# SwiGLU gate and up as two by two blocks with seven products, the down projection in three pieces

## The chip, the cores and the metric

One core of a Trainium2 chip runs the whole kernel. The metric is the device time of one execution in microseconds. Five engines work side by side, each through its own queue in order: TensorE (PE in the profile: matmuls; PEld: the loads of their weights), VectorE (DVE), ScalarE (ACT), GpSimd (POOL) and SyncE (SP, which issues most DMAs). Matmuls write PSUM, eight banks that VectorE and ScalarE read.

## The reference

One decoder layer for 512 prompt tokens and 64 sample tokens (T = 576) of width 1024: a mixer (Mamba-2 heads and mLSTM heads), cross-attention over a memory, and SwiGLU, each between two RMS norms and added to the stream x. The change is in the last part:

```python
x = x + _rms(o) * g_post_x
u = _rms(x) * g_pre_ffn
f = (jax.nn.silu(u @ w_gate) * (u @ w_up)) @ w_down    # 1024 -> 2816 -> 1024
x = x + _rms(f) * g_post_ffn
```

All is float32.

## The kernel before

Activations lie features by tokens: eight tiles of 128 features, 576 tokens. A float32 product is made of three matmuls in the faster fp32r type: each operand is split into a high and a low part, and hi·hi, lo·hi and hi·lo are added in PSUM. A weight tile (128 output features, 1024 input features) is one load of 512 KB into `raw` (two buffers); `split_w` (L170) then makes `whi` by a cast on ScalarE (L177) and `wlo` by a subtraction, the first `cut` columns on VectorE and the others on GpSimd (L184). With `acc` the low part is instead a negated copy by ScalarE (L181), to which a DMA issued by GpSimd adds the weight once more from memory (L182). `whi` and `wlo` have three buffers each, with `NWX` more in a pool `wx` for one stage. `weights` (L1058) keeps the last few split tiles, so that both halves of the tokens use one split.

`gemm` (L191) runs 24 matmuls for one tile and one half of the tokens: eight weight tiles times three (L197, L198, L199). The tokens are cut in `HALVES`, 256 and 320.

The part around the change, in order:

- `xo` (L1364): output projection of the cross-attention for eight tiles, first half, then second half in the order `XO1`. `chain` (L1378) adds the normed result to x and splits it into `u3h` and `u3l`; `pre_sums` adds up squares for the next norm, whose factor comes as `rb3`.
- Tiles 0 to 3 of gate and up (`products` L1398, `hidden` L1404): the first half of the tokens while VectorE still works on the second half of x, then the second half. `hidden` multiplies both products by `rb3` (the norm's factor is applied after the matmul), takes silu of the gate on ScalarE, multiplies on GpSimd and splits the result into `hh` and `hl`.
- The loop over tiles 4 to 21 (`NFFN` is 22), both halves each.
- `down` (L1472): for each of eight output tiles and each half 66 matmuls over all 22 hidden tiles in one PSUM bank, then a square for the last norm and a scaled copy.
- The end: the factor of the last norm for the second half, the last two down products of the first half around it, the additions to x (`post_add`), transposes of the first half (`final0`) and the output DMAs.

The program is written in order, and a scheduler orders each engine's queue by a simulated timeline in which earlier lines have priority; it places tiles into their buffers and adds the waits. `issue_after` holds instructions behind a given one on their engine.

## Time and profile before

| | us |
|---|---|
| median of 3 runs | 1146.4 |
| lowest, highest | 1144.42, 1146.73 |
| profiled execution | 1144.03 |
| its span | 1142.3 |
| TensorE busy (matmuls) | 1127.8 |
| VectorE busy | 631.9 |
| ScalarE busy | 507.7 |
| GpSimd busy | 319.2 |

The span runs from the first instruction to the last; the profiled execution's own time has another 1.7 us around it. The granted clock of TensorE was 0.999 of full speed. Busy times are unions of the time in which an engine had an instruction running, and matmuls overlap each other, so a matmul's own duration is longer than the distance to the next one. In the DMA view a row names destination and source, issuing queue, count, KB of one and the median us from issue to landing.

### The profile page before, as it was taken

What the parts mean: (1) busy time and instruction counts of PE and PEld (TensorE: products, weight loads), DVE (VectorE), ACT (ScalarE), POOL (GpSimd) and SP (SyncE); (2) the same over time, 40 slices, a digit from 0 to 9 for tenths busy, and PEclk for the clock granted to TensorE, in tenths of its full rate; (3) what the DMA queues carried; (4) which work ended last, traced back from release to release, by engine and by line L of the source; (5) the groups of instructions that cost most, each with busy time, mean ns of one, the idle gap of its engine ahead of it and who ended that gap; (6) DMA issues with size and microseconds to landing.
All of it is one profiled execution on the core that took longest, in us unless ns stands there. A gap on an engine that the chain in (4) does not pass through costs nothing.

```text
span 1142.3 us, 21407 instructions
## 1 busy us (share of the span) xinstructions
PE 1127.8 (99%) x8633; PEld 1079.5 (95%) x8633; DVE 631.9 (55%) x1266; ACT 507.7 (44%) x930; POOL 319.2 (28%) x349
## 2 busy tenths in 40 slices
PE   9999999999999999999999999999999999999997
PEld 8999888898998999999888899999999999999997
DVE  6796774558777762568444547834434444311225
ACT  6877533355554463655344455522223232232222
POOL 1333443313122111101343200224433443331330
PEclk9999999999999999999999999999999999999999
DMA  6685565445554432544577733412222233422332
GB/s 213 156 171 126 130 167 165 140 111 142 162 161 123 128 111 84 166 167 157 193 248 249 266 124 97 154 56 78 89 92 75 75 92 93 152 72 82 102 102 97
DMA packets 48023, 153.38 MB, mean 134 GB/s; under 512 B 5260, under 2 KB 9484, under 8 KB 47412
## 3 DMA queue, kind: packets, MB, share of 16 engines
q1 hardware_dynamic: 42164, 139.43, 38.1%
q0 software_dynamic: 5760, 12.59, 6.8%
q8 instruction: 67, 1.10, 0.4%
q14 instruction: 32, 0.26, 0.1%
HBM read 135.54 MB, written 16.45 MB: 133 GB/s over the span
## 4 chain that ended last, share of the span: by engine, by line
PE 87%; DMA 4%; DVE 3%; ACT 3%; issue 1%; SPq 0%; POOL 0%; POOLq 0%; DVEq 0%; ACTq 0%
PE ps_in L197 5%; PE ps_in L199 5%; PE ps_in L198 5%; PE ps_u L199 4%; PE ps_g L199 4%; PE ps_dn L197 4%; PE ps_g L198 4%; PE ps_u L198 4%; PE ps_g L197 4%; PE ps_u L197 4%; PE ps_dn L199 4%; PE ps_dn L198 4%; PE ps_o L199 3%; PE ps_o L197 3%; PE ps_o L198 3%; PE ps_v L770 2%
## 5 line engine op out<-in xcount | busy, mean ns | idle before, releaser
L177 ACT CAST whi<-raw 128x1024 fp32r<-128x1024 f32 (+1 forms) x166 | 171.6, 1036 | 212.9 <-issue 50.4
L184 DVE TENSOR_TENSOR wlo<-raw,whi 128x512 fp32r<-128x512 f32 (+1 forms) x158 | 144.8, 916 | 164.0 <-ACT whi L177 163.3
L184 POOL TENSOR_TENSOR wlo<-raw,whi 128x512 fp32r<-128x512 f32 (+1 forms) x82 | 139.2, 1698 | 237.5 <-ACT whi L177 233.9
L197 PE MATMUL ps_in<-uh,whi 128*128 128x320 f32 (+1 forms) x544 | 165.3, 304 | 0.0
L199 PE MATMUL ps_in<-uh,wlo 128*128 128x320 f32 (+1 forms) x544 | 162.8, 300 | 0.2 <-DVE wlo L184 0.2
L198 PE MATMUL ps_in<-ul,whi 128*128 128x320 f32 (+1 forms) x544 | 162.2, 298 | 0.0
L197 PEld LDWEIGHTS ps_in<-uh,whi 128*128 128x128 f32 x544 | 103.0, 189 | 2.2 <-issue 0.8
L199 PEld LDWEIGHTS ps_in<-uh,wlo 128*128 128x128 f32 x544 | 102.9, 189 | 2.1 <-issue 1.3
L197 PE MATMUL ps_u<-u3h,whi 128*128 128x256 f32 (+1 forms) x352 | 104.3, 296 | 0.0
L199 PE MATMUL ps_g<-u3h,wlo 128*128 128x256 f32 (+1 forms) x352 | 104.3, 296 | 0.0
L199 PE MATMUL ps_u<-u3h,wlo 128*128 128x256 f32 (+1 forms) x352 | 104.3, 296 | 0.0
L197 PE MATMUL ps_g<-u3h,whi 128*128 128x256 f32 (+1 forms) x352 | 104.3, 296 | 0.0
L198 PE MATMUL ps_g<-u3l,whi 128*128 128x256 f32 (+1 forms) x352 | 104.3, 296 | 0.0
L198 PE MATMUL ps_u<-u3l,whi 128*128 128x256 f32 (+1 forms) x352 | 104.2, 296 | 0.0
L197 PE MATMUL ps_dn<-hh,whi 128*128 128x320 f32 (+1 forms) x352 | 104.2, 296 | 0.0
L199 PE MATMUL ps_dn<-hh,wlo 128*128 128x320 f32 (+1 forms) x352 | 103.9, 295 | 0.0
L198 PE MATMUL ps_dn<-hl,whi 128*128 128x320 f32 (+1 forms) x352 | 103.8, 295 | 0.0
L198 PEld LDWEIGHTS ps_in<-ul,whi 128*128 128x128 f32 x544 | 103.1, 189 | 0.7
L199 PEld LDWEIGHTS ps_g<-u3h,wlo 128*128 128x128 f32 x352 | 66.8, 190 | 0.1
L199 PEld LDWEIGHTS ps_u<-u3h,wlo 128*128 128x128 f32 x352 | 66.8, 190 | 0.1
L198 PEld LDWEIGHTS ps_u<-u3l,whi 128*128 128x128 f32 x352 | 66.8, 190 | 0.0
L197 PEld LDWEIGHTS ps_g<-u3h,whi 128*128 128x128 f32 x352 | 66.8, 190 | 0.0
(591 smaller groups left out, 2952.3 us busy)
## 6 DMA issues: line engine op xcount, KB each, us to landing
raw<-win SPq DMA_DIRECT2D x35, 512.0 KB, 3.8
raw<-wgate SPq DMA_DIRECT2D x23, 512.0 KB, 3.5
raw<-wup SPq DMA_DIRECT2D x22, 512.0 KB, 3.6
raw<-wdown SPq DMA_DIRECT2D x18, 512.0 KB, 3.5
raw<-wout SPq DMA_DIRECT2D x17, 512.0 KB, 3.6
kva<-kc SPq DMA_DIRECT2D x16, 512.0 KB, 6.6
kva<-vc SPq DMA_DIRECT2D x16, 512.0 KB, 7.1
raw<-wxq SPq DMA_DIRECT2D x13, 512.0 KB, 3.6
```

Source lines behind the costliest of these rows:

```text
L177: A.copy(hi[:, :n], raw[:, :n])
L184: e.tensor_tensor(lo[:, a:b], raw[:, a:b], hi[:, a:b].bitcast(F32), op=ALU.subtract)
L197: mm(ps, wh, ah, start=i == 0, stop=False)
L198: mm(ps, wh, al, start=False, stop=False)
L199: m = mm(ps, wl, ah, start=False, stop=i == len(tiles) - 1)
L770: m = mm(o, ah, lo[:, j:j + 256], start=False, stop=k == KT - 1, skip_group_check=True)
```

## The change

**Halves.** From the output projection of the cross-attention up to the end of gate and up the tokens are cut 288 and 288 (`EHALVES`), with the norm's transposes in overlapping chunks (`ECHUNKS`).

**Tiles 0 to 3** stay as they were, in another order: tile 3 comes first for its first half, and it is computed for both halves once more behind the sums of blocks.

**Sums of blocks.** x is stored to memory and then scaled in place by gain and norm factor. With four blocks B11, B12, B21, B22 (two halves of the input features by two halves of the tokens) VectorE and ScalarE make the high and low parts of seven operands, `b11`, `b21`, `t1` to `t4`, `b22`.

**Pairs.** Tiles 4 to 21 are taken two at a time. For gate and for up of each pair, a `Pair` loads both weight tiles, forms sums of their blocks on VectorE and splits four operands: `w1` (high part by ScalarE, low part by negation and an accumulating DMA), `w2`, `w3` (one half of its low part by an accumulating DMA) and `w4` of half width. Seven products of 12 matmuls, 288 columns each, replace the 96 matmuls of two tiles and two halves. They go into three PSUM banks; three intermediate sums are copied out by ScalarE and added by VectorE (`done`). On TensorE the order is `early` (two products), `late` of the pair before (two), `mid` (three). GpSimd has no tensor work left here: silu's product is on VectorE.

**Down** goes in three pieces, after hidden tiles 0 to 7, 8 to 15 and 16 to 21. The first piece is copied from PSUM to `f2`, the others are added to it by VectorE. Each piece starts with three partial products that leave out the last two hidden tiles, with `late` of the last pair behind the first of them. The last piece runs all second halves, then all first halves, with the last norm and the additions to x between.

**Room.** Ten small tiles of the mixer and one of the attention move from long-lived pools to those of their stages, and `NWX` goes from 4 to 3.

```diff
@@ -28,6 +28,9 @@
 CHUNKS = [(0, 128), (128, 128), (256, 128), (384, 128), (512, 64)]
 HALVES = [(0, 256), (256, 320)]
 HCHUNKS = [CHUNKS[:2], CHUNKS[2:]]
+EHALVES = [(0, 288), (288, 288)]
+ECHUNKS = [[(0, 128), (128, 128), (160, 128)], [(288, 128), (416, 128), (448, 128)]]
...
-NWX = 4
+NWX = 3
...
-    CT = cp.tile([P, 5, 104], F32, name="CT")
-    cumst = cp.tile([80, T], BF16, name="cumst")
...
+    CT = ml.tile([P, 5, 104], F32, name="CT")
+    cumst = ml.tile([80, T], BF16, name="cumst")
...
-        xo(j, 0, wx if 2 < j < 7 else None)
-    post_rstd(0, ssq, rb, "px0")
+        xo(j, 0, wx if 3 < j < 7 else None)
+    rstd_rows(rstd_cols([ssq], ECHUNKS[0], "px0", alloc=B0), ECHUNKS[0], rb, B0)
     for n_, j in enumerate(XO1):
         xo(j, 1)
         if n_ < 2:
             chain(0, range(4 * n_, 4 * n_ + 4))
         if n_ in (3, 5):
-            pre_sums(0, x, ssq3, range(2 * n_ - 6, 2 * n_ - 2))
-    hh = [SL0("hh0"), SL(2, "hh1", F32R), None]
-    hl = [SL(1, "hl0", F32R), SL(4, "hl1", F32R), None]
-    def products(j, i, up, pool=None, cut=CUT):
-        t0, n = HALVES[i]
+            sums(0, range(2 * n_ - 6, 2 * n_ - 2))
+    S.dma_start(x_d[:, :, E[0]], x[:, :, E[0]])
...
+    psg, m = products(3, 0, 0)
     with tc.issue_after(m.ins):
-        rc = rstd_cols([ssq3], HCHUNKS[0], "p30", alloc=B1)
-    psu, m = products(0, 0, 1, wx, 1024)
+        rc = rstd_cols([ssq3], ECHUNKS[0], "p30", alloc=B1)
+    psu, m = products(3, 0, 1)
...
+    hidden(3, 0, psg, psu)
+    psg, m = products(0, 0, 0, wx)
...
+    hidden(2, 1, psg, psu)
+    for j in (1, 0):
         ffn(j, 1)
     wxs.close()
+    S.dma_start(x_d[:, :, E[1]], x[:, :, E[1]])
     fp = ctx.enter_context(tc.tile_pool(name="ffn", bufs=1, reuse_waits="tile"))
-    tp_ = fp
-    hh[2], hl[2] = [fp.tile([P, 6, T], F32R, name=k) for k in ("hh2", "hl2")]
-    S.dma_start(x_d, x)
-    for j in range(4, NFFN):
-        ffn(j, 0)
-        ffn(j, 1)
-    f = SL(3, "f_ffn")
-    x2 = SL(5, "x2")
+    b4 = SL(4, "b4", F32R, (P, 16, 288))
+    b5 = bx.tile([P, 16, 288], F32R, name="b5", tag="b5")
+    (B11, B12), (B21, B22) = [[x[:, 4 * k:4 * k + 4, c] for c in E] for k in range(2)]
+    for i in range(2):
+        for k in range(KT):
+            V.scalar_tensor_tensor(x[:, k, E[i]], x[:, k, E[i]], PAR("g_preffn", k), rb3[:, E[i]], op0=ALU.mult, op1=ALU.mult)
+    def parts(t_, i, src):
+        hi, lo = [t_[:, 4 * k:4 * k + 4, :] for k in (i, i + 1)]
+        split(hi, lo, src)
+        return hi, lo
+    def minus(out, a, b):
+        V.tensor_tensor(out, a, b, op=ALU.subtract)
+    b11 = parts(b4, 0, B11)
+    minus(B11, B12, B11)
+    t1 = parts(b5, 2, B11)
+    minus(B11, B22, B11)
+    t2 = parts(b5, 0, B11)
+    b21 = parts(b4, 2, B21)
+    minus(B12, B22, B12)
+    minus(B21, B21, B11)
+    ffn(3, 0)
+    ffn(3, 1)
+    b3, bf = SL(3, "b3", F32R, (P, 16, 288)), fp.tile([P, 8, 288], F32R, name="bf")
+    t3, t4, b22 = parts(b3, 0, B12), parts(b3, 2, B21), parts(bf, 0, B22)
+    gs = SL(5, "gs", F32, (P, 16, 288))
+    sw = [gs[:, 8 + 4 * i:12 + 4 * i, :].rearrange("p a b -> p (a b)")[:, 0:1024] for i in range(2)]
+    f2 = SL(1, "f_ffn")
...
+    class Pair:
+        def __init__(s, j, up, hh, hl):
+            s.j, s.up, s.hh, s.hl = j, up, hh, hl
+            src = I["wup" if up else "wgate"]
+            r1 = wp.tile([P, 1024], F32, name="raw", tag="raw", bufs=2)
+            r2 = fp.tile([P, 1024], F32, name="rawx", tag="rawx", bufs=2)
+            st_ = sw[up]
+            S.dma_start(r1, src[j])
+            S.dma_start(r2, src[j + 1])
+            a, b = slice(0, 512), slice(512, 1024)
+            hl_ = lambda p=wp, k=("whi", "wlo"), n=1024, m=3: [p.tile([P, n], F32R, name=q, tag=q, bufs=m) for q in k]
+            w1, w2, w3 = hl_(), hl_(), hl_()
+            w4 = hl_(fp, ("w4h", "w4l"), 512, 2)
+            neg = lambda w, c: A.activation(w[1][:, c], w[0][:, c].bitcast(F32), AF.Copy, scale=-1.0)
+            A.copy(w1[0], r1)
+            neg(w1, slice(0, 1024))
+            G.dma_start(w1[1], src[j], accum_op=ALU.add)
+            V.tensor_tensor(st_[:, b], r2[:, a], r2[:, b], op=ALU.add)
+            V.tensor_tensor(st_[:, a], st_[:, b], r1[:, a], op=ALU.subtract)
+            V.tensor_tensor(r2[:, a], r1[:, a], r2[:, a], op=ALU.subtract)
+            V.tensor_tensor(r1[:, b], r1[:, b], st_[:, a], op=ALU.subtract)
+            split(*w2, st_)
+            A.copy(w3[0], r2)
+            neg(w3, b)
+            G.dma_start(w3[1][:, b], src[j + 1, :, b], accum_op=ALU.add)
+            V.tensor_tensor(w3[1][:, a], r2[:, a], w3[0][:, a].bitcast(F32), op=ALU.subtract)
+            split(*w4, r1[:, b])
+            s.w = w1, w2, w3, w4
+            s.ps = None
+        def bank(s):
+            return (MP if s.up else GP)("ps_u" if s.up else "ps_g")[:, :288]
+        def mul(s, ps, w, i, b, start=True):
+            hi, lo = s.w[w]
+            for k in range(4):
+                wh, wl = [t_[:, 512 * i + k * P:512 * i + k * P + P] for t_ in (hi, lo)]
+                mm(ps, wh, b[0][:, k, :], start=start and k == 0, stop=False, skip_group_check=True)
+                mm(ps, wh, b[1][:, k, :], start=False, stop=False, skip_group_check=True)
+                m = mm(ps, wl, b[0][:, k, :], start=False, stop=k == 3, skip_group_check=True)
+            return m
+        def tmp(s, k):
+            return tp_.tile([P, 288], F32, name=k, tag=k, bufs=3)
+        def done(s, a, i, ps, more=None):
+            g = gates(s.j)[a][i]
+            if not s.up:
+                if more is not None:
+                    V.tensor_tensor(g, ps, more, op=ALU.add)
+                A.activation(g, ps if more is None else g, AF.Silu)
+                return
+            if more is not None:
+                t_ = s.tmp("t2")
+                V.tensor_tensor(t_, ps, more, op=ALU.add)
+                ps = t_
+            V.tensor_tensor(g, g, ps, op=ALU.mult)
+            k = (s.j + a) % 8
+            split(s.hh[:, k, E[i]], s.hl[:, k, E[i]], g)
+        def early(s):
+            s.x, y = s.bank(), s.bank()
+            s.mul(s.x, 0, 0, b11)
+            c = s.tmp("t1")
+            A.copy(c, s.x)
+            s.mul(y, 0, 1, b21)
+            s.done(0, 0, y, c)
+        def mid(s):
+            s.mul(s.x, 1, 0, t2, False)
+            s.c2, c3 = s.tmp("t1"), s.tmp("t1")
+            A.copy(s.c2, s.x)
+            s.z = s.bank()
+            s.mul(s.z, 1, 1, t1)
+            s.mul(s.x, 2, 0, t3, False)
+            A.copy(c3, s.x)
+            s.done(1, 1, s.z, c3)
+        def late(s):
+            s.mul(s.x, 2, 1, t4, False)
+            s.done(1, 0, s.x)
+            s.mul(s.z, 3, 0, b22, False)
+            s.done(0, 1, s.z, s.c2)
+    def pairs(js, hh, hl):
+        last = None
+        for j in js:
+            for up in range(2):
+                p = Pair(j, up, hh, hl)
+                p.early()
+                if last:
+                    last.late()
+                p.mid()
+                last = p
+        return last
+    def down_part(c, nk, j, i, ps, w, k0, k1):
+        t0, n = HALVES[i]
+        return gemm(ps, [(*w, nk)], act(hh), act(hl), t0, n, k0, k1)
+    def down_chunk(c, nk, order, last, w_of, evac):
+        ps, n1 = {}, nk - 2
+        def get(j, i):
+            if (j, i) not in ps:
+                ps[j, i] = (GP if len(ps) < 3 or len(ps) % 2 else MP)("ps_dn")[:, :HALVES[i][1]]
+            return ps[j, i]
+        for n_, (j, i) in enumerate(order[:3]):
+            down_part(c, nk, j, i, get(j, i), w_of(j), 0, n1)
+            if n_ == 0:
+                last.late()
+        for n_, (j, i) in enumerate(order):
+            p = get(j, i)
+            m = down_part(c, nk, j, i, p, w_of(j), n1 if n_ < 3 else 0, nk)
+            evac(n_, j, i, p, m)
+    def ev_first(n_, j, i, ps, m):
+        t0, n = HALVES[i]
+        A.copy(f2[:, j, t0:t0 + n], ps)
+    def ev_add(n_, j, i, ps, m):
+        t0, n = HALVES[i]
+        V.tensor_tensor(f2[:, j, t0:t0 + n], f2[:, j, t0:t0 + n], ps, op=ALU.add)
+    for c, (js, ev) in enumerate((((4, 6), ev_first), ((8, 10, 12, 14), ev_add))):
+        if c:
+            hh, hl = SL0("hh%d" % c), SL(2, "hl%d" % c, F32R)
+        last = pairs(js, hh, hl)
+        w_of = lambda j: weights(("d", j, c), I["wdown"][j, :, 1024 * c:1024 * c + 1024], cut=1024)
+        down_chunk(c, 8, [(j, i) for j in range(8) for i in (1, 0)], last, w_of, ev)
+    hh, hl = SL0("hh2"), SL(2, "hl2", F32R)
+    last = pairs((16, 18, 20), hh, hl)
...
+    wdh = SL(4, "wdh", F32R, (P, 6, 768))
+    wdl = bx.tile([P, 16, 288], F32R, name="wdl", tag="b5").rearrange("p a b -> p (a b)").rearrange("p (j c) -> p j c", c=768)
+    x2 = SL(3, "x2")
     ssqf = ssq_tile("ssqf")
     rb = rb_tile("pf_rb")
-    def down_ws(j, cut):
-        return [(*weights(("d", j, q), I["wdown"][j, :, 1024 * q:1024 * q + 128 * m], 128 * m, cut=min(cut, 128 * m)), m)
-                for q, m in enumerate((8, 8, 6))]
-    HH = lambda k, t0, n: hh[k // 8][:, k % 8, t0:t0 + n]
-    HL = lambda k, t0, n: hl[k // 8][:, k % 8, t0:t0 + n]
-    def down_evac(j):
-        def ev(t0, n, ps):
-            add_sq(ph, ssqf, ps, j, n, t0=t0)
-            A.activation(f[:, j, t0:t0 + n], ps, AF.Copy, scale=PAR("g_postffn", j))
-        return ev
-    def down(j, i, cut=CUT):
-        gemm2(down_ws(j, cut), HH, HL, down_evac(j), "ps_dn", [i], GP if i else MP)
+    kept = {}
+    def w_of(j):
+        if j not in kept:
+            src = I["wdown"][j, :, 2048:2816]
+            kept[j] = split_w(src, 768, 768) if j > 5 else split_w(src, 768, to=(wdh[:, j, :], wdl[:, j, :]))
+        return kept[j]
+    def down_evac(n_, j, i, ps, m):
+        t0, n = HALVES[i]
+        fj = f2[:, j, t0:t0 + n]
+        V.tensor_tensor(fj, fj, ps, op=ALU.add)
+        add_sq(ph, ssqf, fj, n_, n, t0=t0)
+        A.activation(fj, fj, AF.Copy, scale=PAR("g_postffn", j))
+    down_chunk(2, 6, [(j, 1) for j in (6, 7, 0, 1, 2, 3, 4, 5)], last, w_of, down_evac)
+    S.dma_start(x2, x_d)
...
+    for n_, j in enumerate(range(8)):
+        ps = (MP if n_ % 2 else GP)("ps_dn")[:, :256]
+        m = down_part(2, 6, j, 0, ps, w_of(j), 0, 6)
+        down_evac(n_, j, 0, ps, m)
+        if n_ == 1:
+            with tc.issue_after(m.ins):
+                rc = rstd_cols([ssqf], HCHUNKS[1], "pf1", alloc=B0)
+        if n_ == 3:
+            with tc.issue_after(m.ins):
+                rstd_rows(rc, HCHUNKS[1], rb, B0)
+            for k in range(8):
+                post_add(1, f2, x2, rb, [k], False)
+                if k % 2:
+                    S.dma_start(O["y1"][:, k - 1:k + 1, :], x2[:, k - 1:k + 1, 256:T])
```

More of the change, by code (lines that the diff above doesn't have):

```diff
@@ L1430, in build @@
[L1430 to L1444 removed]
+        rstd_rows(rc, ECHUNKS[0], rb3, B1)
```

122 lines of the change are left out of this document (53 added, 69 removed).

## The prediction

> **What bounds the kernel now.** I read the page's engine line and its chain first, then stretches of the span, then single instructions of the SwiGLU and the down projection.
>
> ```profile
> span 1142.3 us, 21407 instructions
> PE 1127.8 (99%) x8633; PEld 1079.5 (95%) x8633; DVE 631.9 (55%) x1266; ACT 507.7 (44%) x930; POOL 319.2 (28%) x349
> ...
> PE 87%; DMA 4%; DVE 3%; ACT 3%; issue 1%; SPq 0%; POOL 0%; POOLq 0%; DVEq 0%; ACTq 0%
> ```
>
> TensorE is busy 99% of the 1142.3 us and carries 87% of the chain. The next fence gives stretches: us, then busy time (and instructions) of each engine.
>
> ```profile
> core 0: us, PE busy (x) PEld busy (x) DVE busy (x) ACT busy (x) POOL busy (x), PEclk, DMA share, GB/s
> 659.00:745.00 86.00, 85.95 (x659) 84.91 (x656) 59.88 (x125) 46.69 (x94) 9.95 (x11) 1.00 0.39 126
> ...
> 760.00:985.00 225.00, 225.00 (x1693) 225.00 (x1693) 94.68 (x140) 64.97 (x105) 87.52 (x70) 1.00 0.27 82
> ```
>
> Row 760 to 985 is the loop over tiles 4 to 21 of gate and up, which the change rewrites. TensorE is busy in all 225.00 us; VectorE in 94.68 (42%), ScalarE in 64.97 (29%), GpSimd in 87.52. Nothing but the matmuls sets the time there, so fewer matmuls are worth their full price as long as the three other engines, which get more to do, never make TensorE wait. Row 659 to 745 is the stage ahead (the cross-attention output, tiles 0 to 3): VectorE is at 59.88 of 86.
>
> Price of a matmul, from the starts of three timeline rows (start, duration, instruction):
>
> ```profile
> 990.21 0.31 PE L197 MATMUL ps_dn<-hh,whi 128*128 128x320 f32 x1
> ...
> 999.89 0.28 PE L197 MATMUL ps_dn<-hh,whi 128*128 128x256 f32 x1
> ...
> 1007.73 0.31 PE L197 MATMUL ps_dn<-hh,whi 128*128 128x320 f32 x1
> ```
>
> Each stretch between them is 22 weight tiles by three matmuls, 66 in all. 320 columns: (999.89 - 990.21)/66 = 0.1467 us. 256 columns: (1007.73 - 999.89)/66 = 0.1188. A width of 288 isn't in the trace; it lies halfway, and I take 0.1327, between those ends.
>
> **The matmuls.** A pair of tiles of one kind (gate or up) costs 2 tiles x 24 matmuls x (0.1467 + 0.1188) = 12.74 us. The seven products are 7 x 4 weight tiles x 3 = 84 matmuls of 288 columns: 84 x 0.1327 = 11.15 us. That is 1.59 less, for nine pairs of tiles and two kinds: 18 x 1.59 = 28.7 us. But the new code computes tile 3 for its first half twice (once at the start, once more in the call after the block sums): 48 x 0.1327 = +6.4 us. The down projection keeps its matmuls, only their order changes. Net on TensorE: **-22.3 us**. All else is waits that come back.
>
> **Load of the other engines, per pair of one kind.** Rows: count, busy us, mean ns.
>
> ```profile
> L177 ACT CAST whi<-raw 128x1024 fp32r<-128x1024 f32 x34 | 35.7, 1050 | 63.6 <-issue 34.3 <-PE ps_g L198 27.3 <-PE ps_u L198 2.1
> ...
> L189 DVE TENSOR_TENSOR hl<-t,hh 128x320 fp32r<-128x320 f32 x18 | 26.4, 1467 | 1.6 <-ACT hh L188 1.6
> ...
> L1408 DVE TENSOR_TENSOR t<-ps_g,p_rb 128x320 f32<-128x320 f32 x17 | 8.3, 490 | 22.0 <-PE ps_g L199 22.0
> ...
> L1410 ACT ACTIVATE t<-t 128x320 f32<-128x320 f32 x17 | 7.9, 467 | 0.0
> ...
> L1408 DVE TENSOR_TENSOR t<-ps_g,p_rb 128x256 f32<-128x256 f32 x18 | 7.4, 412 | 0.3 <-PE ps_g L199 0.3
> ...
> L189 DVE TENSOR_TENSOR hl<-t,hh 128x256 fp32r<-128x256 f32 x17 | 7.2, 424 | 23.5 <-ACT hh L188 23.5
> ```
>
> ```profile
> L184 DVE TENSOR_TENSOR wlo<-raw,whi 128x512 fp32r<-128x512 f32 x22 | 15.9, 721 | 59.0 <-ACT whi L177 59.0
> ```
>
> ```profile
> L184 DVE TENSOR_TENSOR wlo<-raw,whi 128x1024 fp32r<-128x1024 f32 x14 | 17.1, 1223 | 13.8 <-ACT whi L177 13.8
> L1039 DVE SCALAR_TENSOR_TENSOR u3l<-x,par,u3h 128x320 fp32r<-128x320 f32 x8 | 4.4, 598 | 0.0
> ```
>
> ```profile
> L181 ACT ACTIVATE wlo<-whi 128x512 fp32r<-128x512 f32 x32 | 19.8, 626 | 0.3
> ...
> L181 ACT ACTIVATE wlo<-whi 128x1024 fp32r<-128x1024 f32 x8 | 8.4, 1054 | 0.1
> ```
>
> VectorE per pair: six passes of 512 columns (four sums of blocks, two low parts; 721 ns each), one of 1024 (1223 ns), so 5.5 us of weights; a 288-wide pass over PSUM lies between 412 and 490 ns, 0.45: three for gate; three, four products and four low parts for up. So 6.9 us for gate and 10.5 for up, mean 8.7 of 11.15 (78%). ScalarE: four passes of 1024 (1050 and 1054 ns), two of 512 (626 ns), three PSUM copies and four silu or casts (467 ns at 320 columns, so about 0.44): 8.5 us (76%). Both below TensorE, with the up pair close on VectorE; I cost this load at nothing, covered by the gate pair's slack of 4 us, and if that cover goes, VectorE's excess is the price. GpSimd loses its tensor passes in this loop. The two low-part rows (1467 ns at 320 columns, 424 at 256) show VectorE being slowed when GpSimd runs beside it, so this side can also gain a little; off the path, zero.
>
> **The new wait.** There are three buffers of weight parts, and each pair now uses all three (w1, w2, w3). The first block's low part goes ScalarE copy, ScalarE negation, then an accumulating DMA by GpSimd. The same chain stands in the input projection:
>
> ```profile
> 29.50 1.06 ACT whi L177
> 30.59 1.06 ACT wlo L181
> ```
>
> ```profile
> 31.97 1.06 POOL L182 DMA_DIRECT2D wlo<-win  x1 [3.80 <-ACT wlo L181]
> ```
>
> ```profile
> wlo<-win POOLq DMA_DIRECT2D x24, 256.0 KB, 5.7
> ...
> wlo<-win POOLq DMA_DIRECT2D x8, 512.0 KB, 5.6
> ```
>
> ```profile
> DMA to landing us min/median/max: 3.9/5.8/9.3
> ```
>
> The copy starts at 29.50, the negation at 30.59 and the DMA at 31.97 (0.32 after the negation's end); landing takes 5.6 us in the median at 512 KB, 3.9 to 9.3 over all forty. So from a free buffer to a usable low part: 31.97 - 29.50 + 5.6 = 8.1 us. The order on TensorE is first part of pair p (24 matmuls), last part of p-1 (24), middle of p (36), first part of p+1. w1 comes free after the first 24, so its successor has 60 matmuls, 60 x 0.1327 = 7.96 us, plus two before the low part is first read (0.27): 8.2. That is a tie. When a landing is 5.6 or less nothing waits; when it is slower all of it shows, since TensorE's queue is in order and the last part of p, which is ready sooner, stands behind. Bounds: 0 (landing 5.6) to 9.3 - 5.7 = 3.6 us per pair. Half of the landings are above the median; with an average excess of some 1.2 us there, I take 0.6, nearer zero as the median row is. Fifteen times a pair follows a pair; for twelve of them this holds: **+7.2**.
>
> The other three are the second pair of each group (8, 16 and 4 begin a group after other work). There no last part stands between: the buffer has 36 matmuls, 4.78 + 0.27 = 5.05 us, for the 8.1, so 3.1 us short, unless the scheduler puts the last part of the first pair ahead, which fills it. I take half: 3 x 1.55 = **+4.7** (0 to 9.3).
>
> On the Trainium skill: "DMA: Bandwidth & Descriptors", Anatomy of one DMA (the GpSimd path), gives about 2.0 us plus bytes over 436 GB/s, an estimate of 3.2 us for 512 KB. This trace disagrees for the accumulating form: 5.6 us, and 5.7 for half the bytes, and only the shortest of forty comes near. By the skill's figure both items above would be about 0 and the sum -17.3. I go by the rows.
>
> **From tiles 0 to 3 into the pairs.** VectorE gets 16 scalings (below 598 ns, 0.55: 8.8 us), seven low parts of 1152 columns (1.22 x 1152/1024 = 1.38: 9.6) and four differences (5.5), 23.9 us. The last three of the low parts (4.1) stand behind tile 3's last matmul, which frees the two u3 buffers. Ahead of that, from the second half's norm on, lie 192 matmuls (25.5 us) with 8 us of VectorE work of their own, and idle time in the stage before (26 of 86 us). About 19.8 to place in 17.5 plus a part of that idle time: it nearly fits. After the release the first pair needs two block sums, a cast and a low part (0.72 x 2 + 1.05 + 1.22 = 3.7) against 24 matmuls (3.2), behind tile 3's own evacuation. **+3** (0 to 10).
>
> **Tail.** The long passes over x stay, 16 in number:
>
> ```profile
> 1126.07 3.31 DVE L1031 TENSOR_TENSOR f_ffn<-f_ffn,pf_rb 128x320 f32<-128x320 f32 x8 [0.65 <-ACT pf_rb L248]
> 1129.30 3.30 DVE L1032 TENSOR_TENSOR x<-x,f_ffn 128x320 f32<-128x320 f32 x8
> ```
>
> 3.31 + 3.30 = 6.6 us. They now share VectorE with two passes (0.42 each) for each of four evacuations: 10.0 us against four groups of 18 matmuls at 0.1188, 8.6. With one more addition in the last evacuation: **+2** (0 to 4). The added sums of the first two down pieces (0.45 each) hide behind 24 matmuls (2.8 us or more). One more reload of an output weight hides in the stage that has VectorE and ScalarE idle; uncovered it is 2.3. The extra accumulating traffic, 18 x 768 KB = 13.8 MB, goes into a loop whose DMA share is 0.27.
>
> **Sum.** -22.3 + 7.2 + 4.7 + 3 + 2 = **-5.4 us**. The profiled execution took 1144.0 (span 1142.3), the median of the runs is 1146.4, 0.2% above. Carried to the median: **1141.0**. About 0.2% (2.3 us) is what a measurement of this kernel can tell from no change.
>
> **Rivals.** First, the cycle of the w1 buffer as the bound, slower than before. w3 of a pair asks for a buffer earlier in the program than w1 of the next. If it takes the one that the first part frees, w1 must wait for the one that the last part frees halfway: 12 matmuls in, 48 left, 6.37 + 0.27 = 6.6 us for 8.1. That is 1.5 more, twelve times: +18, 1159. It decides from 0.45 us per pair upwards (5.4/12): beyond that the change loses. For it: the tie above, and a median landing that half of the DMAs exceed; against it: if w3 is early, the last part is ready early too, and could be placed first.
>
> Second, VectorE as the bound of the transition: 23.9 us found covered only by halves, 10 us more than I took, 1151. For it: 78% load with in-order queues behind waiting evacuations; against it: 26 idle us in the stage ahead.
>
> Third, the gain comes through: all landings near the shortest (3.9), the chain 6.4, no wait in the twelve, 1.35 in the three: -22.3 + 4 + 3 + 2 = -13.3, 1133. Against it stands the median of forty, nearly 2 us longer. The Trainium skill's figure, named above, would have it so.
>
> That the change doesn't do what it says is out: the counts of matmuls are in the code.
>
> **How the numbers follow.** Forecast 0.45 (its own range 1130 to 1152, from 0 to 1.5 us per pair), first rival 0.30 (1150 to 1168), second 0.12 (1146 to 1158), third 0.13 (1127 to 1136). Range 1127 to 1163, which leaves out the far end of the first rival and little else. Faster by over 0.2% (below 1144.1): 0.7 of the forecast plus the third, 0.45. Within: 0.18 of the forecast, 0.08. Slower: 0.47.
>
> **What would show it.** The pair loop's matmuls at 84 per pair, 288 wide, starting 0.133 us apart (a width dearer than halfway would undo the saving directly). Then TensorE's idle time in that loop, in the list of waits, put down to the accumulating DMA into the low part: 7 us right, 0 the third rival, 20 and more the first. Idle time at the first pairs put down to ScalarE or VectorE instead, over 8 us, is the second. The forecast is wrong if VectorE or ScalarE is above 90% in the loop, or if the stages ahead of 650 us, which only have tiles moved between pools, take another time.

## The result, and the profile after

The changed kernel takes 1184.3 us (median of 4 runs, 1179.05 to 1188.19) against 1146.6 for the kernel before in the same session: 1.033 times as long, interval 1.0287 to 1.0373. The forecast was 1141, its range ended at 1163. The profiled execution took 1183.3 us.

The page of the profile after, engine line:

```profile
span 1181.5 us, 21257 instructions
PE 1123.5 (95%) x8471; PEld 1067.5 (90%) x8471; DVE 722.1 (61%) x1437; ACT 594.2 (50%) x1082; POOL 227.8 (19%) x289
```

TensorE has 162 matmuls fewer and is busy 4.3 us less, but in a span that is 39.2 us longer. With the 22.3 us that the matmuls should save, some 61.5 us of loss are to be found. Stretches of the span after, cut at the borders of the stages: the last products of x and tiles 0 to 3; group 1 (four pairs); down; group 2 (eight pairs); down; group 3 (six pairs); down and the end. Columns as before: us, busy time of each engine, granted clock, DMA share.

```profile
core 0: us, PE busy (x) PEld busy (x) DVE busy (x) ACT busy (x) POOL busy (x), PEclk, DMA share, GB/s
655.00:774.20 119.20, 115.38 (x868) 111.24 (x867) 84.96 (x165) 60.51 (x114) 16.69 (x14) 1.00 0.43 138
774.20:831.70 57.50, 45.16 (x303) 42.62 (x302) 38.31 (x60) 32.33 (x53) 8.35 (x9) 0.91 0.49 118
831.70:887.40 55.70, 55.70 (x423) 55.70 (x422) 17.78 (x23) 17.62 (x30) 0.86 (x1) 1.00 0.34 97
887.40:995.10 107.70, 91.64 (x638) 89.34 (x637) 56.24 (x98) 57.28 (x98) 13.01 (x15) 0.95 0.54 127
...
1050.90:1122.40 71.50, 64.37 (x470) 62.50 (x469) 39.89 (x69) 41.74 (x71) 9.52 (x11) 1.00 0.55 124
1122.40:1156.30 33.90, 32.90 (x239) 32.64 (x238) 18.27 (x33) 15.94 (x31) 0.00 (x0) 1.00 0.38 136
1156.30:1181.50 25.20, 17.02 (x134) 15.91 (x132) 14.34 (x39) 8.44 (x18) 2.83 (x3) 0.84 0.26 94
```

The three groups are 300, 636 and 468 matmuls long (the last 36 of each lie within the next down piece), which at 0.1333 us is 40.0, 84.8 and 62.4. So group 1 loses 17.5 us, group 2 22.9 and group 3 9.1, together 49.5. In group 2, 16.1 of it is idle time (107.70 - 91.64). The other 6.8 are busy time above the price of the matmuls: about 4.5 in three stretches at a lower clock (one of them is shown below; the row's clock is 0.95), the rest at the eight restarts after waits. Group 3, with a clock of 1.00, has 2.0 of such busy time too (64.37 - 62.4). The down stretch between them is at its price. From 1122.4 to the end are 59.1 us for matmuls worth 43.0, so 16.1 are something else; from the first down product of the kernel before to its end it was 152.1 - 140.2 = 11.9. That makes 4.2 more at the end. The remaining 7.8 us lie ahead of the first pair.

TensorE's list of waits (us in total, times, longest):

```profile
PE ps_u L1540 <- DMA wlo<-wup: 14.2, 6, 3.5
PE ps_g L1540 <- DMA wlo<-wgate: 8.7, 6, 2.2
PE ps_g L1538 <- ACT whi L191: 7.5, 4, 4.6
```

The accumulating DMA is waited for 22.9 us, where the prediction had put 7 for its forecast and "20 and more" for the first rival. The third line is ScalarE's; 4.55 of its 7.5 us are at the first pair and 1.51 at the third. With VectorE's low parts (1.13 and 1.06) and three shorter waits, group 1 has 10.2 us of waits for these two engines, and the prediction's sign for the second rival was over 8. So both signs were there.

One cycle of group 2. First TensorE's timeline, then ScalarE's and GpSimd's (start, duration):

```profile
922.61 0.32 PE L1538 MATMUL ps_u<-b,whi 128*128 128x288 f32 x1
922.77 0.29 PE L1539 MATMUL ps_u<-b,whi 128*128 128x288 f32 x1
926.41 0.40 PE L1540 MATMUL ps_u<-b,wlo 128*128 128x288 f32 x1 [3.35 <-DMA wlo<-wup]
926.65 0.29 PE L1538 MATMUL ps_u<-b,whi 128*128 128x288 f32 x1
...
927.71 0.67 PE L1540 MATMUL ps_u<-b,wlo 128*128 128x288 f32 x2
928.18 0.44 PE L1538 MATMUL ps_u<-b,whi 128*128 128x288 f32 x1
...
931.07 0.33 PE L1538 MATMUL ps_g<-b,whi 128*128 128x288 f32 x1
```

```profile
914.46 1.05 ACT L1523 CAST whi<-rawx 128x1024 fp32r<-128x1024 f32 x1 [0.50 <-ACT hh L191]
...
916.42 1.05 ACT L1515 CAST whi<-raw 128x1024 fp32r<-128x1024 f32 x1
...
917.71 1.06 ACT L1514 ACTIVATE wlo<-whi 128x1024 fp32r<-128x1024 f32 x1
```

```profile
919.06 0.86 POOL L1517 DMA_DIRECT2D wlo<-wup  x1 [1.52 <-ACT wlo L1514]
```

The first part of the gate pair, whose waiting matmul started at 911.60, ends by 914.4. At 914.46 ScalarE casts w3 (L1523), not the next w1: w3 has taken the freed buffer (the trace names no buffers; the first experiment tests this reading). w1's cast (L1515) starts at 916.42, when the last part of the pair before is through half of its 24 matmuls. That is the order of the first rival. From there the low part needs 10.0 us, not 8.1: the DMA starts 2.64 us after the cast (2.47 was reckoned), and its data is used 7.35 us later, at 926.41. TensorE stands still for 3.35. Then TensorE pays again: from 927.71 to 931.07 the matmuls are 0.24 apart instead of 0.133, 14 of them, 1.5 us.

Not every cycle is as long: of the twelve in which TensorE waits for this DMA, seven take 7.9 to 8.2 us from the cast to the use, and three, this one among them, 9.7 to 10.3.

### The profile page after: what moved, and what is told of

Read it like the earlier page. It is cut to its first block, busy times and chain, and to the rows that moved or that the text cites. A ratio compares the mean times of both kernels' runs of the same rounds, so it can differ in the third digit from the quotient of the medians.

```text
span 1181.5 us, 21257 instructions
## 1 busy us (share of the span) xinstructions
PE 1123.5 (95%) x8471; PEld 1067.5 (90%) x8471; DVE 722.1 (61%) x1437; ACT 594.2 (50%) x1082; POOL 227.8 (19%) x289
## 5 line engine op out<-in xcount | busy, mean ns | idle before, releaser
L180 ACT CAST whi<-raw 128x1024 fp32r<-128x1024 f32 (+1 forms) x125 | 130.3, 1044 | 135.4 <-PE ps_dn L201 29.2
L187 DVE TENSOR_TENSOR wlo<-raw,whi 128x1024 fp32r<-128x1024 f32 (+2 forms) x117 | 118.1, 1009 | 105.0 <-ACT whi L180 101.4
L1540 PE MATMUL ps_u<-b,wlo 128*128 128x288 f32 x216 | 64.7, 312 | 15.4 <-DMA wlo<-wup 14.2
L1538 PE MATMUL ps_g<-b,whi 128*128 128x288 f32 x216 | 64.9, 302 | 7.5 <-ACT whi L191 7.5
L1540 PE MATMUL ps_g<-b,wlo 128*128 128x288 f32 x216 | 62.7, 302 | 9.8 <-DMA wlo<-wgate 8.7
L1538 PE MATMUL ps_u<-b,whi 128*128 128x288 f32 x216 | 66.0, 307 | 2.1 <-ACT whi L191 1.3
L1539 PE MATMUL ps_g<-b,whi 128*128 128x288 f32 x216 | 64.7, 300 | 0.8 <-DVE b L192 0.8
L1539 PE MATMUL ps_u<-b,whi 128*128 128x288 f32 x216 | 65.3, 303 | 0.0
L1540 PEld LDWEIGHTS ps_u<-b,wlo 128*128 128x128 f32 x216 | 41.8, 198 | 18.0 <-DMA wlo<-wup 16.2
L201 PEld LDWEIGHTS ps_dn<-hl,whi 128*128 128x128 f32 x280 | 52.8, 189 | 0.0
L202 PEld LDWEIGHTS ps_dn<-hh,wlo 128*128 128x128 f32 x280 | 52.6, 188 | 0.0
L200 PEld LDWEIGHTS ps_dn<-hh,whi 128*128 128x128 f32 x280 | 52.3, 188 | 0.0
```

The lines of the kernel that those rows point to most:

```text
L180: A.copy(hi[:, :n], raw[:, :n])
L187: e.tensor_tensor(lo[:, a:b], raw[:, a:b], hi[:, a:b].bitcast(F32), op=ALU.subtract)
L200: mm(ps, wh, ah, start=i == 0, stop=False)
L201: mm(ps, wh, al, start=False, stop=False)
L202: m = mm(ps, wl, ah, start=False, stop=i == len(tiles) - 1)
L1538: mm(ps, wh, b[0][:, k, :], start=start and k == 0, stop=False, skip_group_check=True)
```

## The experiments

Theory A: the loss is w1's low part by the accumulating DMA, because of its place in the cycle, plus VectorE's and ScalarE's work on the block sums ahead of the first pairs. Theory B, the rival: the pairs are dear in themselves (load of VectorE and ScalarE, DMA traffic, the down projection in pieces), and taking that wait away brings the next one.

Each ratio is to the kernel before in the same session. That kernel's median lay between 1146.6 and 1148.3 us over the sessions, so 1 or 2 us between kernels of different sessions say nothing.

### The next pair's loads and w1 first

```diff
+        nxt = Pair(*todo[0], hh, hl)        # now loads and w1 alone
...
-                p = Pair(j, up, hh, hl)
+                p = nxt
+                if n_ + 1 < len(todo):
+                    nxt = Pair(*todo[n_ + 1], hh, hl)
+                p.rest()                    # w2, w3, w4
                 p.early()
```

> The loads and the first block w1 of the next pair are asked for ahead of w2, w3 and w4 of this pair; nothing else changes. Theory A (TensorE waits because w1 gets its buffer only halfway through the last part of the pair before, and then needs copy, negation and accumulating DMA, 8 us): w1 now gets a buffer some 96 matmuls ahead of its use, 12.8 us, so the waits on the accumulating DMA (23 us) and the slow clock behind them go; 1150 to 1162 us. Theory B (the queues of VectorE and ScalarE in the pair loop are what is late, the DMA only ends last): stays within 6 us of 1184.

1163.5 us, ratio 1.0138 (1.0114 to 1.0162): 1.5 above theory A's range, 20.8 less than the changed kernel, with the same instructions in another order. Its stretches for the three groups:

```profile
777.90:833.10 55.20, 44.93 (x302) 43.66 (x301) 38.20 (x60) 31.19 (x50) 7.91 (x9) 0.91 0.53 124
889.00:979.60 90.60, 85.94 (x639) 84.81 (x638) 56.41 (x97) 56.53 (x95) 12.11 (x14) 1.00 0.65 148
1035.60:1100.40 64.80, 63.06 (x470) 62.35 (x469) 39.72 (x68) 40.91 (x69) 8.63 (x10) 1.00 0.59 130
```

Group 2 loses 5.8 instead of 22.9, group 3 2.4 instead of 9.1, and the clock is back at 1.00. The DMA share in group 2 is 0.65, above the 0.54 of the changed kernel, so the traffic isn't what cost the time. The waits for the accumulating DMA are halved (11.6 us for 22.9). Group 1 still loses 15.2; two waits for the DMA there make 5.2 of it (3.76 and 1.46), and the longest of the others (3.74) is for ScalarE.

### w1's low part by VectorE, in the changed kernel's order

```diff
-            neg(w1, slice(0, 1024))
-            G.dma_start(w1[1], src[j], accum_op=ALU.add)
+            V.tensor_tensor(w1[1], r1, w1[0].bitcast(F32), op=ALU.subtract)
```

> The low part of w1 is a VectorE subtraction of 1024 columns in place of ScalarE's negation and the accumulating DMA. Theory A: the chain shrinks from 8 to about 2.5 us, the waits go, 1148 to 1162 us although VectorE gets 1.2 us more per pair (10 of 11.2). Theory B: VectorE is the bound, 18 x 1.2 us more on it, 1184 to 1205 us.

1170.4 us, ratio 1.0199 (1.0175 to 1.0223). Above theory A's range, well below B's. The chain is shorter, but starts as late, and now stands in VectorE's queue:

```profile
PE ps_g L1539 <- DVE wlo L1516: 6.7, 4, 2.8
PE ps_u L1539 <- DVE wlo L1516: 5.5, 5, 1.8
```

The order alone had brought back 20.8 us, this edit brings 13.9. That isn't the price of the DMA, since it puts waits in VectorE's queue in its place; the next run leaves the DMAs out.

### Both accumulating DMAs left out

> Leaves out the two accumulating DMAs of each pair, so the low parts of w1 and of half of w3 hold the negated high parts; all else runs. It prices the DMA alone. Theory A: 1148 to 1158 us, with the waits of the first pairs of the loop (16 us of loss before the first down piece, of which about 4 by the DMA) still there. Theory B: above 1175 us.

1143.5 us, ratio 0.9974 (0.9956 to 0.9992): 40.8 less than the changed kernel, below theory A's range. w1 still gets its buffer late here: without the DMA the late buffer costs nothing in groups 2 and 3, so it is the two together that cost. Groups 2 and 3 (from the down products on) are at their price now, 84.4 us for 84.8 and 62.2 for 62.4. The first row is group 1 without its first 21 matmuls:

```profile
776.10:822.90 46.80, 40.98 (x279) 40.11 (x278) 36.15 (x55) 30.36 (x48) 1.74 (x1) 0.89 0.29 91
878.80:963.20 84.40, 84.40 (x638) 84.40 (x637) 56.40 (x98) 57.91 (x97) 0.00 (x0) 1.00 0.30 94
1019.20:1081.40 62.20, 62.20 (x470) 62.20 (x469) 39.83 (x69) 42.14 (x70) 0.00 (x0) 1.00 0.24 74
```

ScalarE and VectorE have the same load per pair as in the changed kernel, so their load costs nothing in these two groups, as the prediction had it. Of waits in the pairs only the first pair's are left, the longest of 4.5 us for `whi`. Group 1 loses 46.8 - 37.2 = 9.6, so about 8 of its 17.5 go with the DMAs and about 10 don't.

### Tile 3's first half computed once

```diff
-    ffn(3, 0)
     ffn(3, 1)
```

> Tile 3's first half is computed once, at the start, and not again behind the sums of blocks. If TensorE sets the time there, 48 x 0.133 = 6.4 us less, 1178 us. If VectorE's sums of blocks set when the pairs can begin, the matmuls were cover and the time stays at 1184 within 2 us.

1182.0 us, ratio 1.0299 (1.0257 to 1.0341), 2.3 under the changed kernel. The runs of both spread over 9 us or more, so the medians decide neither for 0 nor for 6.4. The trace is clearer: without these matmuls TensorE's wait at the first pair grows from 4.55 to 5.76 us, the next one for a low part by VectorE from 1.13 to 2.06, and more of group 1 runs at the lower clock. From the last product of an earlier stage (`ps_xq`, in the cross-attention) to the first down product it saves 1.4 us of the 6.4. So they were mostly cover.

### Next pair first, and w1's low part by VectorE

> The next pair's loads and first low part go ahead of this pair's, as in the run with that order alone (1163.5 us), and in addition w1's low part is a subtraction by VectorE. Theory A (the wait is a matter of w1's accumulating DMA, 5.4 us from issue to landing, within the pair's cycle): with the next pair's low part made a whole pair ahead, the rest of the DMA waits on line 1545 (11.6 us in 7 waits) goes, 1150 to 1156 us. Rival: the order already hid the DMA in the steady stretch, and 1.35 us of VectorE per pair in the same queue as the SwiGLU products delay those instead: 1162 to 1172 us, with waits on VectorE in the place of those on the DMA.

1159.4 us, ratio 1.0135 (1.0095 to 1.0175): not to be told from the order alone. Neither range was met. In its trace waits for VectorE's low part (3.4 us in four) have come in place of some of those for the DMA, and the ones at the first pair are left.

### Ordinary tiles 4 to 7 ahead of the first pair

```diff
-    ffn(3, 0)
-    ffn(3, 1)
+    for j in (3, 4, 5, 6, 7):
+        for i in range(2):
+            if (j, i) != (3, 0):
+                ffn(j, i)
...
-    for c, (js, ev) in enumerate((((4, 6), ev_first), ((8, 10, 12, 14), ev_add))):
+    for c, (js, ev) in enumerate((((), ev_first), ((8, 10, 12, 14), ev_add))):
```

> The order of the run at 1163.5 us; tiles 4 to 7 of gate and up go by the ordinary 96 matmuls per tile half, tile 3's first half isn't computed twice, and the pairs begin at tile 8, so that the sums of blocks of x are made beside the ordinary tiles. Lost: 4 pairs of the saving, 4 x 1.59 = 6.4 us; gained: 6.4 us of repeated matmuls, and the stall in which TensorE waits for those sums. Theory A (transition: about 10 us of idle and of slow clock in 774 to 835 us go): 1150 to 1155 us. Rival (the VectorE work only moves its stall to the ordinary tiles, whose products and casts it does too): 1160 to 1166 us.

1147.0 us, ratio 0.9998 (0.9971 to 1.0024), 16.6 less than with pairs from tile 4, better than the theory's range. In place of group 1's stretch stands one without a gap:

```profile
774.00:835.00 61.00, 61.00 (x460) 61.00 (x460) 38.57 (x51) 22.80 (x34) 14.51 (x9) 1.00 0.30 87
```

The gain of four pairs (6.4 us) was given up, as many matmuls of tile 3 fell away, and the transition's loss went.

### The same with w1's low part by VectorE, or without accumulating DMAs

> The kernel with the ordinary tiles 4 to 7 and the next pair's loads first, with w1's low part a subtraction by VectorE instead of a negation and an accumulating DMA. Theory A: the last DMA waits go, 1144 to 1150 us if the ordinary tiles do take the transition away. Rival (VectorE delays the products): no better than the same kernel with the DMA, within 3 us or above it.

1145.0 us, ratio 0.9984 (0.9968 to 1.0), within both theories, so this run doesn't decide between them.

> The kernel with the ordinary tiles 4 to 7 and the next pair's loads first, with the pairs' two accumulating DMAs left out (the low parts of w1 and w3 are then only the negated high parts). It shows what is left of the saving with neither transition nor DMA: 14 pairs x 1.59 = 22.3 us of matmuls less than the kernel before, and three down pieces. Theory A: 1146.7 - 22.3 + about 6 of tail = 1128 to 1134 us. Rival (something else than these two holds the time, a slower clock or the loads): above 1140 us.

1133.2 us, ratio 0.9894 (0.9874 to 0.9915), as the theory had it: 14 pairs without the DMAs bring a little over 1%, with the waits ahead of the pairs (told below) still in it.

### w1's low part by GpSimd, or split

```diff
-            neg(w1, slice(0, 1024))
-            G.dma_start(w1[1], src[j], accum_op=ALU.add)
+            G.tensor_tensor(w1[1][:, a], r1[:, a], w1[0][:, a].bitcast(F32), op=ALU.subtract)
+            G.tensor_tensor(w1[1][:, b], r1[:, b], w1[0][:, b].bitcast(F32), op=ALU.subtract)
```

> The kernel with the ordinary tiles 4 to 7 and the next pair's loads first (1147.0 us), with w1's low part by GpSimd, two subtractions of 512 columns at 1.75 us each, instead of the negation and the accumulating DMA (5.4 us). Theory A (that landing is what the pairs still wait for): the low part stands 3.5 us after the cast instead of 6.5 to 7 us, the waits of about 6 us in the 14 pairs go, 1139 to 1144 us. Rival (the low part isn't ready in time this way either, or VectorE is slowed beside GpSimd): 1145 us or more, with TensorE waiting for GpSimd's or VectorE's instructions.

> As the kernel with w1's low part by GpSimd, but the half of the columns that TensorE needs first is subtracted by VectorE and the other half by GpSimd: 0.7 us and 1.75 us side by side. Theory A: the waits go, 1139 to 1144 us. Rival (VectorE's queue, with the instructions of the other pair ahead, delays its half): 1144 to 1147 us, as where VectorE did it all (1145.0 us).

1145.9 us, ratio 0.9975 (0.9959 to 0.9992), and 1145.5, ratio 0.9981 (0.9966 to 0.9997): the rivals' numbers. The intervals of all four forms of the low part overlap, the accumulating DMA's (0.9971 to 1.0024) included. With GpSimd's, TensorE waits for w3's accumulating DMA instead (1.7 us at the longest; GpSimd had been idle before it issued that one, so it was not late through GpSimd's work); with the split, VectorE's half is waited for.

### The down projection in three pieces alone

All tiles by the ordinary matmuls, no sums of blocks.

> The other part of the change alone: all tiles of gate and up by the ordinary 96 matmuls, no sums of blocks, the down projection in three pieces with its partial results added by VectorE. It has the matmuls of the kernel before. Theory: the pieces cost only what the end loses (about 6 us: the last piece's tiles end with an addition, a square and a product, and the products of tile pairs stand before them), so 1148 to 1154 us. Rival: the pieces themselves cost more, in waits for the last hidden tiles at three places and in loads of down's weights for each piece: 1156 to 1165 us; then part of the loss of 37.6 us was theirs and not the pairs'.

1149.6 us, ratio 1.001 (0.9995 to 1.0025): 1.4 us more than before (-0.6 to +2.9). The pieces cost 3 us at most, so all but that of the loss is the pairs' and the sums of blocks'. In its trace the end loses 2.9 us more than before, near the prediction's 2. The trace shows one thing more. Stretches around 740 us: kernel with three pieces, then kernel with the split low part:

```profile
735.00:745.00 10.00, 9.61 (x72) 9.37 (x71) 9.79 (x24) 5.91 (x15) 2.93 (x2) 1.00 0.33 118
745.00:755.00 10.00, 10.00 (x79) 10.00 (x78) 6.24 (x12) 4.26 (x7) 0.85 (x1) 1.00 0.32 107
```

```profile
735.00:745.00 10.00, 7.32 (x44) 6.43 (x44) 10.00 (x26) 5.65 (x15) 3.52 (x2) 0.92 0.22 82
745.00:755.00 10.00, 10.00 (x71) 10.00 (x70) 9.36 (x16) 6.31 (x11) 0.00 (x0) 0.91 0.18 63
```

115 matmuls against 151 in 20 us. VectorE is full or nearly so in both from 735 to 745; in the second kernel it has done this just before:

```profile
729.09 4.63 DVE L1470 SCALAR_TENSOR_TENSOR x<-x,par,p_rb 128x288 f32<-128x288 f32 x8
733.64 1.55 DVE L1387 TENSOR_TENSOR f_xo<-f_xo,px_rb 128x288 f32<-128x288 f32 x4
```

Eight scalings of x for the sums of blocks (L1470), ready early and wanted late, stood ahead of the residual chain of the second half (L1387), which tiles 0 to 2 wait for. The changed kernel has the same waits at that place (0.85, 0.48 and 1.31), 2.6 us, and the kernel with three pieces only 0.39.

### The scaling held back

```diff
+    chained = chain(1, range(4, 8))         # returns its last instruction
...
+    with tc.issue_after(chained.ins):
+        for i in range(2):
+            for k in range(KT):
+                V.scalar_tensor_tensor(x[:, k, E[i]], x[:, k, E[i]], ...
```

On the kernel with the split low part:

> The kernel with ordinary tiles 4 to 7, the next pair's loads first and w1's low part split between VectorE and GpSimd (1145.5 us); in addition the 16 instructions that scale x for the sums of blocks (8 for each half of the tokens, 4.6 us of VectorE together for a half) are held behind the last instruction of the second half's residual chain. In the trace without this they run at 729.1 us, ahead of that chain, and TensorE then waits 2.6 us at 740 and runs at half clock to 749. Theory: those eight are what it waits for, the stretch from 735 to 755 us loses 5 us less, 1139 to 1142 us. Rival (the chain's own length sets that wait, or the instructions only delay another thing): 1144 to 1147 us.

On the changed kernel:

> The changed kernel (1184.3 us) with that one edit: the 16 instructions that scale x are held behind the residual chain of the second half. Theory: 5 us go at 740, but the sums of blocks then come 4 to 5 us later and the first pair with them, so that most is given back in the transition: 1180 to 1185 us. Rival (the sums have time enough): 1177 to 1180 us.

1144.0 us, ratio 0.9974 (0.9959 to 0.9989), and 1190.7, ratio 1.0373 (1.0351 to 1.0395). Both theories' numbers failed. The first run came out at its rival's, and not to be told from the kernel without the edit (0.9966 to 0.9997): the wait at 740 is gone (0.39 left), but the scaling now stands ahead of the sums of squares, and TensorE waits for the norm's factor at 761:

```profile
PE ps_rb L250 <- DVE p_r L239: 1.9, 1, 1.9
```

The changed kernel came out 6.4 us slower by the medians, 0.4% by the ratios, whose intervals overlap; 1190.7 is above both ranges. The first pair starts 2.7 us later, counted from the last `ps_xq` product, so more was lost at 763 than the wait at 740 had cost; group 1 takes 57.5 us as before. In group 3, which the edit doesn't touch, the waits for the accumulating DMA grew as well (3.43 and 3.19 us at the longest, 1.9 before). Why there is open.

### Held behind the sums of squares too, and no accumulating DMA

```diff
-    with tc.issue_after(chained.ins):
+    with tc.issue_after(held.ins):          # first product of tile 2's second half
```

> As the kernel with the scaling of x held back (1144.0 us), but held behind the first product of tile 2's second half, so behind the sums of squares of the second half as well: in the trace of that kernel the scaling and two sums of blocks stood ahead of those sums, and TensorE waited 1.86 and 0.98 us at 761 us in place of 740. Theory (VectorE's order is all that this stretch loses): gate and up to the first down piece take 102 to 103 us as with three pieces alone, in place of 105.4, and the time is 1140 to 1142 us. Rival: the held work meets tiles 3 and 4 and delays those: 1144 us or more.

1140.4 us, ratio 0.9939 (0.9924 to 0.9954), as the theory had it: faster than the kernel before and than the same kernel held less far (0.9959 to 0.9989). Its stretches around 740 us, then groups 2 and 3:

```profile
735.00:745.00 10.00, 9.60 (x73) 9.37 (x72) 10.00 (x25) 6.68 (x16) 2.08 (x2) 1.00 0.15 53
745.00:755.00 10.00, 10.00 (x78) 10.00 (x77) 8.72 (x17) 4.06 (x8) 1.75 (x2) 1.00 0.23 74
871.40:959.90 88.50, 86.07 (x639) 84.85 (x638) 64.25 (x103) 50.27 (x89) 16.11 (x14) 1.00 0.41 114
1015.90:1080.70 64.80, 63.10 (x470) 62.34 (x469) 44.96 (x72) 36.63 (x66) 11.40 (x10) 1.00 0.37 95
```

VectorE's order was what the stretch at 740 lost. The groups still lose 3.7 and 2.4 us.

The last run takes w1's low part to GpSimd and w3's wholly to VectorE:

> The same order, and no accumulating DMA in the pairs at all: w1's low part by GpSimd (two subtractions, 1.75 us each), w3's low part wholly by VectorE (1.2 us instead of 0.7 and a negation and a DMA). Theory: GpSimd has nothing else in the pairs, so its low part is there in time, the waits on w1 in the pairs (4 to 5 us in the traces with a share of VectorE) go, 1137 to 1140 us. Rival (VectorE, or GpSimd's 3.5 us, ends as late as before): within 2 us of the kernel with the split low part.

1142.0 us, ratio 0.9956 (0.994 to 0.9973): the rival, 1.6 us from the run before. The waits are now for w2's low part (L192), 5.1 us in eight, where the run before waited 3.9 us in six for VectorE's half of w1's: VectorE's queue is what both end in.

## Why the prediction was wrong

**The matmuls: right.** 288 columns take 0.133 us, 84 per pair and kind; the run without accumulating DMAs shows both long groups at exactly that. 162 fewer in the trace are 18 x 12 saved less 48, as counted, and a few records missing. What was wrong in this term is +6.4 for tile 3: on TensorE, yes, but in a place where it would mostly have waited anyway (1.4 us back in the trace when it is left out).

**The wait per pair: the step that failed most.** "That is a tie", and 0.6 us per pair taken as the nearer end. The two long groups lose 32.0 us, for which the sum had 9.1. The step that failed is the buffer: I took the order in which w1 gets the buffer that the first part frees, and left the other to a rival at 0.30. The program requests w3 of a pair before w1 of the next, and the trace follows the program; the code was there to be read. So w1 had not 60 matmuls but 48, as that rival had it, and the 8.1 us of the chain were right for most cycles: in group 3 they are 7.9 to 8.2, and its four waits (1.88, 1.47, 1.40, 1.17) are 1.5 us in the mean, the rival's price to the tenth. Two things came on top. In three up pairs of group 2 the chain takes 9.7 to 10.3 us, because of the landing (7.35 in the cycle shown); why it is longer there is not shown. The medians, first for gate, then for up:

```profile
wlo<-wgate POOLq DMA_DIRECT2D x9, 512.0 KB, 5.4
...
wlo<-wup POOLq DMA_DIRECT2D x9, 512.0 KB, 6.0
```

And a long wait's price is more than its length: the three of 2.98 to 3.50 us in group 2 are each followed by matmuls at a lower clock, about 1.5 us each. The sum had nothing for that. By order alone (next pair first) 20.8 us come back.

**From tiles 0 to 3 into the pairs.** For group 1 the sum had 3 + 1.55 + 1.2 = 5.8 us; it loses 17.5. About 8 of it go with the accumulating DMAs; the 9.6 that are left without them are in the second rival's place. The forecast had 3 for it and that rival 13. VectorE's timeline in the changed kernel:

```profile
763.70 2.65 DVE L1470 SCALAR_TENSOR_TENSOR x<-x,par,p_rb 128x288 f32<-128x288 f32 x6
...
777.18 1.35 DVE L1478 TENSOR_TENSOR x<-x 128x1152 f32<-128x1152 f32 x1
778.45 1.95 DVE L192 TENSOR_TENSOR b<-x,b 128x1152 fp32r<-128x1152 f32 x1
780.32 0.68 DVE L1519 TENSOR_TENSOR gs<-gs,raw 128x512 f32<-128x512 f32 x1
```

The sum of weight blocks at 780.32 (L1519), of which ScalarE makes w2's high part, stands behind a difference and a low part of x, and TensorE waits 4.55 us for it at 782. "It nearly fits" had too much time in it. It put 192 matmuls (25.5 us) between the second half's norm and the release; but TensorE runs many of them ahead of the norm's factor, and from the first scaling of the second half (762.64) to the first pair (774.23) there are 11.6 us. From 763.70 to 782.10 VectorE is busy 17.60 of 18.40 us, so there was no room left. With ordinary tiles 4 to 7 beside the same work, the loss was gone.

**The end: right in kind.** +2 forecast (0 to 4); 2.9 with the pieces alone, 4.2 in the changed kernel, just beyond the range, one of it a wait for `wdh`.

**Not in the sum: 7.8 us ahead of the pairs.** 2.6 is the wait at 740, which the prediction passed over ("idle time in the stage before (26 of 86 us)" was taken as room for that very work). Another 3.5 lie ahead of the last `ps_xq` product, which starts at 622.75 us in the trace before and at 626.25 after. The prediction named this as a sign of being wrong. And 1.1 is a wait of the output projection (`ps_xo`) for ScalarE's copies, which the trace before doesn't have. Before, then after:

```profile
300.00:400.00 100.00, 97.92 (x719) 93.18 (x718) 74.90 (x210) 49.76 (x109) 19.70 (x24) 1.00 0.51 141
```

```profile
300.00:400.00 100.00, 98.02 (x712) 93.28 (x711) 73.27 (x208) 48.10 (x106) 19.75 (x24) 0.98 0.49 139
```

The clock in that stretch is 0.98 after and 1.00 before, and TensorE waits 1.3 us for a load of `h` in place of 0.2. Two kernels derived from the changed one (no accumulating DMAs; next pair first with VectorE's low part), whose code is the same up to there, have 1.00 in that stretch and start that product at 623.73 and 623.09; the other derived kernels have 0.97 or 0.98 and start it between 624.7 and 631.0. So the 3.5 us vary between traces of the same code, and about 1 of them at most is a fixed cost of the tiles moved between pools. The trace before is also one of the faster executions of its kernel (1144.0 us, median 1146.4).

**The rivals.** The first had the right mechanism (1159), the second the right place (1151), and each was priced as if the other didn't happen. Both did. Together, 18 and 10 us more than the forecast, they give 1169; the result is beyond that too, by what the sum had at nothing: the time ahead of the pairs, the lower clock, the longer landings.

**What stays open.** In the best kernel the sum would be 14 x 1.59 = 22.3 saved, less 6.1 in the groups and 3 to 4 at the end: about 12 us faster. 6.5 are measured. Its trace starts the last `ps_xq` product at 631.0 us, 8.3 later than the trace before, with clocks of 0.97 and 0.98 from 200 to 400 us where the other has 1.00; from that product to the end it is 10.1 us faster. So most of the missing time lies ahead of the change, in how these two executions ran. Whether other executions of the two kernels differ in the same way is not shown. Open too is why the landings for up in group 2 are longer, and whether the waits that are left can be had out of VectorE's queue.

## What to carry to other kernels

With a ring of as many buffers as one step requests, the order of the requests can set the wait: write down who takes each freed buffer before pricing a chain, and ask for the longest chain first. A queue with idle time is no room for early work: instructions that are ready early and wanted late go ahead of those that are wanted now, unless they are held back. And where two rivals can both happen, price them together.

## What the hardware showed

A wait of TensorE can cost more than itself. After the idle 3.35 us the matmuls were 0.24 us apart instead of 0.133 for 3.36 us (927.71 to 931.07), beginning 1.3 us after the restart. The granted clock from 926.41 to 930.50 was 0.66 in the mean, which is 1.00 up to 927.71 and 0.5 from there. Waits of 2.98 and 3.50 in the same group were followed by the same (after the longer one it began at once), waits of 2.21 and less were not. Three short waits in a row (0.86, 0.48, 1.31 us at 739 to 742) gave a clock of 0.92 in the kernel with the split low part and 1.00 in the changed kernel, with the same waits. The Trainium skill, "TensorE: Matmul & The Clock Gate", Part 1, describes a gate that halves the clock after an idle window of about 3.4 us, a window that runs freely and is not started by the kernel; the traces agree in that the slow stretch lasts as long as one such window and that equal waits can fall on either side, but not in the length of the wait: 2.98 us were enough here.

The accumulating DMA of 512 KB takes 5.4 to 6.0 us in the median from issue to landing in groups with a DMA share of 0.49 to 0.55. The Trainium skill, "DMA: Bandwidth & Descriptors", Anatomy of one DMA, gives a fit that comes to about 3.2 us, an estimate; the rows of the changed kernel disagree with it for this form, as those of before did.
